# A 8192 x 8192 float32 transpose: column strips with staggered store windows and 16 KB SBUF runs

## The chip, the cores and the metric

The kernel runs on one core of one Trainium2 chip. The metric is the device time of one execution in microseconds (us), as the median over runs. The profile is of one execution of the program, taken by the hardware profiler.

A core has a matrix engine (TensorE, PE in the profile), two engines that copy here (VectorE, DVE, and ScalarE, ACT), GpSimd (POOL), which only builds an identity matrix, and SyncE (SP), which here only issues transfers. Data moves between the off-chip memory (HBM) and the on-chip memory (SBUF, 128 partitions) through 16 DMA engines. TensorE writes its results into a small memory of its own, PSUM, from which an engine has to copy them into SBUF.

## The reference

```
def setup_inputs():
    return {
        "x": np.random.randn(8192, 8192).astype(np.float32),
    }

def reference(x: np.ndarray) -> np.ndarray:
    return np.transpose(x)
```

The input has 268.44 MB, and so has the output. Every byte is read once from HBM and written once to it.

## The kernel before

The matrix is cut into blocks of 1024 rows by 2048 columns (`I` by `J`); there are 8 by 4 of them. The outer loop runs over the column blocks, the inner one over the row blocks. A block is one input tile `in_tile` of 128 partitions by 8 rows by 2048 columns (64 KB in each partition). Two of them take turns. It is loaded by two transfers of 4 MB on SyncE's queue (L55): each takes four groups of 128 rows, and a partition receives from each group one run of 8 KB.

The block is then worked off in four groups of four column slices. For each column slice of 128 columns, TensorE transposes eight squares of 128 x 128 (L63) into a PSUM tile `ps` of 128 x 1024, with the identity as the other operand. Four such PSUM tiles, of two banks each, take turns. A whole PSUM tile is copied into a quarter of an `out_tile`, alternately by ScalarE (L69) and VectorE (L71). When four quarters are there, ScalarE's queue issues one store of 2 MB (L76). In it, each partition holds four output rows of 1024 elements, so each run is 4 KB both in SBUF and in HBM; the four rows of a partition lie 128 output rows (4 MB) apart. Four `out_tile` buffers take turns.

All semaphores and the buffers' addresses are chosen by the tile framework. An engine waits where its next instruction needs a tile that is not there or not free: a load waits for the transposes of the block two before it, a transpose waits for the copy that frees its PSUM tile, a copy waits for the store that frees its `out_tile`. The loads have SyncE's queue to themselves; the stores share ScalarE's instruction stream with half of the copies.

Of the kernel before, what the change touches and what calls it, by code (L numbers as in the profile page):

```python
# [1 line left out]

# [5 lines left out]


@with_exitstack
def kernel(
    ctx: ExitStack,
    tc: tile.TileContext,
    x: bass.AP,
    out: bass.AP,
):
    nc = tc.nc
    P = 128
    N, M = x.shape  # L20
    assert x.shape == out.shape[::-1]

    dt = x.dtype

    R = 8
    C = 16
    I = R * P
    J = C * P
    G = 4
    LS = 2  # L30

    const_pool = ctx.enter_context(tc.tile_pool(name="const", bufs=1))
    in_pool = ctx.enter_context(tc.tile_pool(name="in_pool", bufs=2))
    out_pool = ctx.enter_context(tc.tile_pool(name="out_pool", bufs=4))
    psum_pool = ctx.enter_context(tc.tile_pool(name="psum", bufs=4, space=bass.MemoryType.PSUM))

    ident = const_pool.tile([P, P], dt)
    make_identity(nc, ident)

    n_bi = N // I  # L40
    n_bj = M // J

    copy_idx = 0

    for bj in range(n_bj):
        j0 = bj * J
        for bi in range(n_bi):
            i0 = bi * I

            in_tile = in_pool.tile([P, R, J], dt)  # L50
            rs = R // LS
            for s in range(LS):
                src = x[i0 + s * rs * P:i0 + (s + 1) * rs * P, j0:j0 + J]
                src = src.rearrange("(a p) j -> p a j", p=P)
                nc.sync.dma_start(out=in_tile[:, s * rs:(s + 1) * rs, :], in_=src)  # L55

            for g in range(C // G):
                out_tile = out_pool.tile([P, G, I], dt)
                for bb in range(G):
                    b = g * G + bb  # L60
                    ps = psum_pool.tile([P, R * P], dt)
                    for a in range(R):
                        nc.tensor.transpose(  # L63
                            ps[:, a * P:(a + 1) * P],
                            in_tile[:, a, b * P:(b + 1) * P],
                            ident,
                        )
                    if copy_idx % 2 == 0:
                        nc.scalar.copy(out=out_tile[:, bb, :], in_=ps)  # L69
                    else:  # L70
                        nc.vector.tensor_copy(out=out_tile[:, bb, :], in_=ps)  # L71
                    copy_idx += 1

                dst = out[j0 + g * G * P:j0 + (g + 1) * G * P, i0:i0 + I]
                dst = dst.rearrange("(b q) i -> q b i", q=P)
                nc.scalar.dma_start(out=dst, in_=out_tile)  # L76


# [1 line left out]
_INS = ['x']  # L80
_OUTS = [((8192, 8192), 'float32')]


# [23 lines left out]
```

## Time and profile before

| What | Value |
|---|---|
| Median of 10 runs | 1278.55 us (1277.35 to 1280.78) |
| Profiled execution, device time | 1280.58 us |
| Profiled execution, span from first to last instruction | 1278.8 us |
| Mean granted TensorE clock | 0.732 of full speed |
| TensorE matmul busy | 702.9 us (55%), 4096 instructions |
| VectorE busy | 313.5 us (25%), 256 instructions |
| ScalarE busy | 252.9 us (20%), 257 instructions |
| DMA, moved over the span | 537.49 MB, mean 420 GB/s |

Busy time is the sum over an engine's own instructions; an engine that waits is not busy. The DMA rows count packets, the pieces in which the 16 DMA engines move data; a queue's share is the time that its packets took, as a share of 16 times the span. The queue q1 carries the loads and q10 the stores. "Idle before" in a group's row is the time for which its engine stood still just ahead of it, with what released it. In the row of slices the span is cut into 40 equal parts, and 9 means busy for 90% or more.

### The profile page before, as it was taken

How to read it: one execution, taken by the hardware profiler on the slowest of the kernel's cores; microseconds unless marked ns; L12 is line 12 of the kernel's file. 1: busy time of each engine (PE TensorE's matmuls, PEld its weight loads, DVE VectorE, ACT ScalarE, POOL GpSimd, SP SyncE). 2: the span in 40 equal slices, each digit the busy share in tenths (PEclk: the TensorE clock that was granted, in tenths of full speed). 3: DMA queues.
4: the chain of work that ended last, by engine and by line, in shares of the span. 5: the costliest groups of instructions: out<-in, count | busy, mean ns of one | idle time of the engine just before them, and what ended most of it. 6: DMA issues, size and time to landing. Idle time of an engine off the chain costs nothing.

```text
span 1278.8 us, 9511 instructions
## 1 busy us (share of the span) xinstructions
PE 702.9 (55%) x4096; PEld 632.4 (49%) x4096; DVE 313.5 (25%) x256; ACT 252.9 (20%) x257; POOL 0.7 (0%) x6
## 2 busy tenths in 40 slices
PE   4565556555565545655456555465554655556553
PEld 3454445454455544645446444464544655445453
DVE  1222223222232212222122222222222222222222
ACT  1221112121121212212122121212212122121211
POOL 0000000000000000000000000000000000000000
PEclk8767777766777677786677776877667776777767
DMA  9999999999999999999999999999999999999998
GB/s 393 425 422 425 424 424 425 422 423 422 424 423 422 423 424 424 423 422 420 425 424 422 423 424 424 423 422 423 421 425 423 422 423 422 424 423 422 423 422 342
DMA packets 101418, 537.49 MB, mean 420 GB/s; under 512 B 3072, under 2 KB 3072, under 8 KB 68608
## 3 DMA queue, kind: packets, MB, share of 16 engines
q10 hardware_dynamic: 67584, 268.44, 51.3%
q1 hardware_dynamic: 33792, 268.44, 49.6%
q8 instruction: 32, 0.52, 0.1%
q14 instruction: 10, 0.08, 0.0%
HBM read 268.44 MB, written 268.44 MB: 420 GB/s over the span
## 4 chain that ended last, share of the span: by engine, by line
DMA 89%; PE 6%; DVE 3%; issue 0%; ACT 0%; DVEq 0%; ACTq 0%; SPq 0%
DMA out_dram<-out_tile 87%; PE ps L63 6%; DVE out_tile L71 3%; DMA in_tile<-in_x_dram 2%; ACT out_tile L69 0%; DVEq L71 0%; ACTq L69 0%; SPq L55 0%
## 5 line engine op out<-in xcount | busy, mean ns | idle before, releaser
L63 PE MATMUL ps<-ident,in_tile 128*128 128x128 f32 x4096 | 702.9, 345 | 559.9 <-DVE out_tile L71 534.6
L63 PEld LDWEIGHTS ps<-ident,in_tile 128*128 128x128 f32 x4096 | 632.4, 182 | 630.1 <-DVE out_tile L71 603.8
L71 DVE COPY out_tile<-ps 128x1024 f32<-128x1024 f32 x256 | 313.5, 1225 | 950.5 <-DMA out_dram<-out_tile 596.7
L69 ACT COPY out_tile<-ps 128x1024 f32<-128x1024 f32 x256 | 251.6, 1014 | 1008.6 <-DMA out_dram<-out_tile 845.1
L69 ACT ACT_TABLE_LOAD x1 | 1.3, 1283 | 0.7 <-PEq L91 0.7
masks.py:199 POOL TENSOR_SCALAR_AFFINE_SELECT ident<-ident 128x128 f32<-128x128 f32 x1 | 0.3, 292 | 0.1
masks.py:197 POOL MEMSET ident<- 128x128 f32 x1 | 0.2, 204 | 0.3 <-POOLq L91 0.3
L91 POOL MEMSET const-bfloat16-1.0<- 128x1 bf16 x1 | 0.1, 101 | 0.0
L91 POOL MEMSET const-uint8-127<- 128x1 uint8 x1 | 0.1, 101 | 0.0
L91 POOL MEMSET const-float32-0.0<- 128x1 f32 x1 | 0.1, 98 | 0.2 <-issue 0.2
L91 POOL MEMSET const-float32-1.0<- 128x1 f32 x1 | 0.1, 98 | 0.0
## 6 DMA issues: line engine op xcount, KB each, us to landing
in_tile<-in_x_dram SPq DMA_DIRECT2D x64, 4096.0 KB, 28.0
out_dram<-out_tile ACTq DMA_DIRECT2D x128, 2048.0 KB, 29.3
```

The source lines that it names most:

```text
L63: nc.tensor.transpose(ps[:, a * P:(a + 1) * P], in_tile[:, a, b * P:(b + 1) * P], ident,)
L69: nc.scalar.copy(out=out_tile[:, bb, :], in_=ps)
L71: nc.vector.tensor_copy(out=out_tile[:, bb, :], in_=ps)
L91: nc = _bacc.Bacc("TRN2", target_bir_lowering=False, num_devices=1)
```

## The change

The program is written anew, with fixed buffers and hand-placed semaphores inside one critical section of the framework. The computation per square (a TensorE transpose, then a copy out of PSUM) stays.

- The matrix is cut into two strips of 4096 columns. A strip is read in 64 chunks of 128 rows: one load of 2 MB per chunk, 16 KB per partition in one run. Three input buffers take turns.
- A chunk has 32 squares, in eight groups `q` of four (`B = 4`). The four squares of a group go into one PSUM bank of 128 x 512; eight banks take turns. Even groups are copied by ScalarE, odd ones by VectorE.
- Each group collects its squares in a region of SBUF (`reg`, 16 KB per partition; nine of them) over a window of eight chunks. The windows of the eight groups are staggered by one chunk: at the start of a strip group 0's window has one chunk, group 1's two, and so on; after that one group closes at every chunk. At the last chunk of a strip all eight close.
- When a group closes, its region is stored: 128 partitions, four output rows each, of 4 KB for a full window. The SBUF side of the store is described as one run of 16 KB per partition, the HBM side as four rows of 4 KB (`wide_dma`). The first store alone is an ordinary one.
- Loads and stores are all issued by SyncE, on one queue. In its order of instructions, a chunk's store comes ahead of the load of the chunk three later.
- A tensor `pad` of 128 B per partition is placed ahead of the identity and the buffers.

```diff
+def physical(ap):
+    t = ap.tensor
+    dims = [list(d) for d in ap.ap]
+    if len(dims) == 2:
+        dims.insert(1, [dims[1][1], 1])
+    return mybir.PhysicalAccessPattern(
+        ap=dims, offset=ap.offset, dtype=ap.dtype,
+        memref=t.name, memsetref=t.name + "_set",
+    )
+
+def wide_dma(nc, eng, queue, out, in_):
+    return eng.add_instruction(
+        mybir.InstDMACopy(
+            mode="Copy",
+            name=nc.get_next_instruction_name(),
+            engine=eng.engine,
+            ins=[physical(in_)],
+            outs=[physical(out)],
+            queue=queue,
+        )
+    )
...
-    R = 8
-    C = 16
-    I = R * P
-    J = C * P
-    G = 4
-    LS = 2
...
+    S = 32
+    B = 4
+    W = 8
+    NR = S // B
+    NIN = 3
+    NREG = 9
+    NPS = 8
+    CH = N // P
+    J = S * P
+
+    with tc.tile_critical():
+        nc.alloc_sbuf_tensor("pad", [P, 32], dt)
+        ident = nc.alloc_sbuf_tensor("ident", [P, P], dt).ap()
+        ins = [nc.alloc_sbuf_tensor(f"in{k}", [P, J], dt).ap() for k in range(NIN)]
+        regs = [nc.alloc_sbuf_tensor(f"reg{k}", [P, B * W * P], dt).ap() for k in range(NREG)]
+        pss = [nc.alloc_psum_tensor(f"ps{k}", [P, B * P], dt).ap() for k in range(NPS)]
...
+        chunks = [(s, c) for s in range(M // J) for c in range(CH)]
+
+        def load(t):
+            s, c = chunks[t]
+            nc.sync.dma_start(
+                out=ins[t % NIN], in_=x[c * P:(c + 1) * P, s * J:(s + 1) * J]
+            ).then_inc(s_ld[t % NIN], 16)
+
+        for t in range(NIN):
+            load(t)
...
+        for t, (s, c) in enumerate(chunks):
+            nc.tensor.wait_ge(s_ld[t % NIN], 16 * (t // NIN + 1))
+            closing = []
+            for q in [(c + k) % NR for k in range(NR)]:
+                if q not in window:
+                    end = min(c + (q - c) % W, CH - 1)
+                    r = free.pop(0)
+                    window[q] = (c, end, r)
+                    if stored[r]:
+                        (nc.scalar, nc.vector)[q % 2].wait_ge(s_st[r], 16 * stored[r])
+                c0, end, r = window[q]
+                rows = (end - c0 + 1) * P
+                view = regs[r][:, :B * rows].rearrange("p (b i) -> p b i", b=B)
+                ps = pss[n % NPS]
+                e = q % 2
+                if bank[n % NPS] is not None:
+                    nc.tensor.wait_ge(*bank[n % NPS])
+                for b in range(B):
+                    last = nc.tensor.transpose(
+                        ps[:, b * P:(b + 1) * P],
+                        ins[t % NIN][:, (q * B + b) * P:(q * B + b + 1) * P],
+                        ident,
+                    )
+                last.then_inc(s_pe, 1)
+                n += 1
+                o = view[:, :, (c - c0) * P:(c - c0 + 1) * P]
+                i = ps.rearrange("p (b i) -> p b i", b=B)
+                (nc.scalar, nc.vector)[e].wait_ge(s_pe, n)
+                if e == 0:
+                    cp = nc.scalar.copy(out=o, in_=i)
+                else:
+                    cp = nc.vector.tensor_copy(out=o, in_=i)
+                cp.then_inc(s_cp[e], 1)
+                copied[e] += 1
+                bank[(n - 1) % NPS] = (s_cp[e], copied[e])
+                if c == end:
+                    closing.append((q, e, copied[e]))
+            for q, e, count in closing:
...
+                nc.sync.wait_ge(s_cp[e], count)
+                if stores:
+                    st = wide_dma(nc, nc.sync, "qSPDynamicHW", dst, regs[r][:, :B * rows])
...
+                st.then_inc(s_st[r], 16)
...
+                free.append(r)
+            if t + NIN < len(chunks):
+                nc.sync.wait_ge(s_pe, n)
+                load(t + NIN)
```

## The prediction

> **What bounds the kernel now.** I read the page's slices and DMA queues first, then the chain and the waits, then the DMA view in three windows: loads alone, the steady middle, stores alone.
>
> ```profile
> DMA  9999999999999999999999999999999999999998
> DMA packets 101418, 537.49 MB, mean 420 GB/s; under 512 B 3072, under 2 KB 3072, under 8 KB 68608
> q10 hardware_dynamic: 67584, 268.44, 51.3%
> q1 hardware_dynamic: 33792, 268.44, 49.6%
> DMA out_dram<-out_tile 87%; PE ps L63 6%; DVE out_tile L71 3%; DMA in_tile<-in_x_dram 2%; ACT out_tile L69 0%; DVEq L71 0%; ACTq L69 0%; SPq L55 0%
> L63 PE MATMUL ps<-ident,in_tile 128*128 128x128 f32 x4096 | 702.9, 345 | 559.9 <-DVE out_tile L71 534.6
> L71 DVE COPY out_tile<-ps 128x1024 f32<-128x1024 f32 x256 | 313.5, 1225 | 950.5 <-DMA out_dram<-out_tile 596.7
> ```
>
> The 16 DMA engines are full from the first slice to the last. The chain is 87% stores. VectorE (DVE) waits 596.7 us for stores to free `out_tile`; TensorE (PE) waits 534.6 us for VectorE. All waiting ends at the DMA engines, so compute counts for nothing until it exceeds its cover. The only ways down are less engine time for each byte, and less idling at the two ends.
>
> The queue rows give the price of a packet: q1 (loads) 0.496 x 16 x 1278.8 us over its 32768 packets of 8 KB (the other 1024 are the small ones, 16 per DMA, counted as nothing) is 309.7 ns; q10 (stores) likewise 160.2 ns for each of 65536 packets of 4 KB. Two 4 KB packets cost 320.4, so a packet carries a fixed part: 2 x 160.2 - 309.7 = 10.7 ns. Records overlap a little (the shares add to 100.9%), so I also take it from rates. The next three answers are windows 6 to 22, 640 to 960 and 1250 to 1270 us:
>
> ```profile
> DMA packets 853, 6.80 MB, mean 425 GB/s; under 512 B 23, under 2 KB 23, under 8 KB 23
> ...
> DMA packets 25606, 135.37 MB, mean 423 GB/s; under 512 B 777, under 2 KB 777, under 8 KB 17403
> ...
> DMA packets 2103, 8.37 MB, mean 418 GB/s; under 512 B 63, under 2 KB 63, under 8 KB 2102
> ```
>
> Loads alone run at 425 GB/s, or 16 x 8192 / 425 = 308.4 ns a packet; stores alone at 418, or 156.8 ns; the fixed part is 5.2 ns. The ends, windows 0 to 24 and 1262 to 1279 us, 40 slices each:
>
> ```profile
> GB/s 0 0 0 259 341 423 423 437 437 423 437 437 410 437 410 410 423 437 423 437 437 423 423 423 410 437 423 423 437 423 437 410 410 423 410 423 437 410 410 423
> ...
> GB/s 424 386 443 434 395 414 434 414 405 424 424 424 414 414 424 424 386 443 434 395 395 318 289 251 174 125 135 135 125 106 96 67 58 58 29 19 19 0 0 0
> ```
>
> The start loses 2.2 us (9.27 MB moved by 24 us, which take 21.8 at 425). The end loses 6.1 us: the last 17 us move 4.57 MB, 10.9 us of work at 420, because the 16 engines run dry one after another. So 8.3 us are ends, and 1270.5 us are 537.49 MB at 423 GB/s.
>
> **The change, part by part.**
>
> Descriptors. A load of 16 KB runs has 1024 packets per engine instead of 2048 (268.44 MB / 16 / 16384); stores that read 16 KB runs have 1024 reads per engine where there were 4096, with four written rows to each. Price of a 16 KB packet: from the rates, 4 x (308.4 - 156.8) + 5.2 = 611.6 ns; from the records, 4 x (309.7 - 160.2) + 10.7 = 608.7 ns. Neither knows of alignment, which the diff changes too: ahead of the old tiles lie four constants of 32 B and the identity's 512 B per partition, so by my count they start 128 B past a multiple of 256; the `pad` of 128 B makes that 256.
>
> Here the Trainium skill decides between the two. "DMA: Bandwidth & Descriptors", in "Why small descriptors are slow" and "How a descriptor splits into AXI transactions", counts 32 B beats: about 3 cycles on top for each packet, and for a start off a 256 B boundary the beats of the bytes before it, here 4. At the 850 MHz of "Where 436 GB/s comes from" that is 135 beats = 158.8 ns for 4 KB and 263 = 309.4 ns for 8 KB. The trace's 160.2 and 309.7 agree to 1%, though it can't say how much of the fixed part is alignment. By the rule an aligned 16 KB packet is 515 beats = 605.9 ns, by the trace's rates alone 611.6; the page's ceiling of 435 GB/s, an estimate for the lower end, is 602.4. I take 605.9, since it explains both rows, and keep both ends. 2048 packets x 605.9 = 1240.9 us of full engines (1233.7 to 1252.6), against 1270.5 now.
>
> More, smaller DMAs. Loads go from 64 of 4 MB to 128 of 2 MB. Stores go from 128 to 142: per strip one closes at each of chunks 0 to 62, and eight at chunk 63. So 270 DMAs against 192. A rule speaks against this: "SBUF — State Buffer", "The DMA setup-cost knee", puts about 2 us on every DMA; 78 more in series would add 156 us. The row: the window from 6 to 22 us holds the seam between the first and second load of one queue and still averages 425, and four store seams fit in the 418. So a seam costs nothing while something is queued behind it; the small packet at each end of a DMA is at most 78 x 10.7 ns = 0.8 us, which I add.
>
> Short stores. The staggered windows make 28 of the 142 stores short, with rows of 512 B to 3.5 KB (29.4 MB in all). They write 896 rows per engine where full rows would be 448: 448 x 5.2 = 2.3 us if each row is paid, 0 if only the read run is. I take 1, and keep 0 to 5, since no row of the trace shows 512 B writes.
>
> One queue. Stores move from ScalarE's queue (ACTq, 0.38 us an issue) to SyncE's, behind a wait for the closing copy; behind each store waits the next load. 270 issues at 0.4 to 0.9 us are up to 240 of 1250 us for SyncE, free of the path. The load for chunk t+3 goes when PE has done chunk t. When a load lands, its ring still holds two stores and two loads (8 MB, 19 us at 423). PE has 5.8 us of busy time per chunk (702.9 / 4096 = 172 ns x 32); even at the slow pace the timeline shows (24 transposes in 4.54 us) it is 6.1 us. So at least 10 us of queue remain, and PE, 32 transposes per 9.7 us, stays under 65%. Copies are halved in width and doubled in number: 1225 / 2 and 1014 / 2 ns plus some 60 ns, four each per chunk, under 3 us. The PSUM handoffs, now 1024 over eight single banks with hand-written waits, and the ninth store region are hidden by the same 10 us. The region needed by the last copy of a chunk is stored two chunks earlier and lands about 5 to 7 us into the chunk; that copy may wait 1 to 2 us, with only the next chunk's copies behind it.
>
> Strip change. Chunk 64 needs eight regions at once, held by the closing stores (36 x 256 KB = 9.4 MB, 22 us). PE stops, but two loads and those stores are in the ring, and when they end a third and fourth load (10 us) are there; PE catches up in about 3 us. Cost 0 (up to 5).
>
> Ends. First load at 0.7 us as now; chunk 0 lands at about 8 us and, at the timeline's first pace (16 transposes in 3.65 us), frees the next load at about 15.3, when the ring is full until 17: 0, with 2 us at risk. At the end 22 us of stores stand queued; the engines' unequal end stays: 6.1 us.
>
> Sum: 1240.9 + 0.8 + 1 + 8.3 = 1251.0 us of span. The profiled execution took 1280.58 for a span of 1278.8 (+1.8), the runs' median 1278.55 is 2.0 under that; so span and median are within 0.2: **1251 us**, 2.2% faster.
>
> **The rivals.** (1) Stores pay for each 4 KB row written, and alignment is worth nothing to them: 1024 x 605.9 + 4096 x 156.8 = 1262.7, plus 8.3, 0.8 and 2.3: 1274. For it: nothing in the trace shows a run that differs between its two sides. Against: the beat count fits, and aligned rows alone, at 152.1 ns, would already give 1254.
> (2) Slower: one ring for both directions. Before, loads and stores had a ring each; now each engine turns from reading HBM to writing it in one ring, 256 times. If a turn drains the ring, the gain of 27.5 us is gone from 0.11 us a turn; at 0.25 us the time is 1315. Against: the engines now alternate directions at nearly every packet, over 60,000 times, and 423 lies between 425 and 418. That those turns are between two rings leaves this open.
> (3) Loads starve in the first chunks or at the strip change: 5 to 15 us, so 1256 to 1266. My timeline leaves 2 us at the start and several later.
> (4) The wide store is split back into 4 KB descriptors: as (1), or 1254 with alignment.
>
> **How the numbers follow.** The likeliest case has 0.70 (1244 to 1262, from the bounds of the packet and the short stores); rivals 1 and 4 0.12, rival 3 0.08, rival 2 0.10. The range 1243 to 1274 takes in all but rival 2 and stragglers. A difference under 0.2% (2.6 us) can't be told from none; part of rival 1 falls there. Faster 0.86, same 0.04, slower 0.10.
>
> **What would show it.** Right: a load packet near 606 ns, 16384 load packets of 16 KB, about 431 to 433 GB/s in the middle, PE waiting for loads. Stores: few 16 KB packets at 432 (mine) or 4 KB packets near 157 (rival 1). Dips in GB/s at each seam mean rival 2; slices under 9 in the first 30 us or near 630, rival 3. I am wrong if the middle stays at or below 425.

## The result, and the profile after

The changed kernel takes 1266.05 us (median of 9 runs, 1265.58 to 1269.74) against 1278.6 us for the kernel before on the same chips (median of 31). The ratio is 0.9905, with a 95% interval of 0.9896 to 0.9913: 0.95% faster. Forecast were 1251 us and 2.2%. The direction was right and 1266 lies in the range of 1243 to 1274, but the gain is less than half of the forecast one. The profiled execution took 1265.90 us for a span of 1264.1 us.

First the page of the changed kernel: slices, DMA packets, the one queue, the chain, and two of the costliest groups.

```profile
DMA  9999999999999999999999999999999999999998
GB/s 380 418 429 428 429 428 430 428 428 428 427 429 428 429 430 431 427 429 429 428 416 428 430 428 429 430 429 430 428 428 429 430 429 429 427 430 429 430 430 355
DMA packets 39308, 537.51 MB, mean 425 GB/s; under 512 B 4320, under 2 KB 4832, under 8 KB 6240
q1 hardware_dynamic: 39264, 536.89, 100.0%
DMA in<-in_x_dram 76%; PE ps L131 20%; DMA out_dram<-reg 2%; DVE reg L144 0%; ACT reg L142 0%; SPq L197 0%; SPq L68 0%; ACTq L140 0%
L131 PE MATMUL ps<-ident,in 128*128 128x128 f32 x4096 | 726.2, 360 | 510.6 <-DMA in<-in_x_dram 495.7
L144 DVE COPY reg<-ps 128x512 f32<-128x512 f32 x512 | 353.5, 692 | 883.7 <-PE ps L131 850.6
```

The DMA engines are as full as before. What changed is the number of packets, 39308 for 101418, and the middle's rate. The waiting has turned round: TensorE now waits for loads (495.7 us of its 510.6 idle), where it waited for copies that waited for stores. That is a change of where the backlog stands, not of what bounds: one full set of DMA engines, before and after.

The rate of the middle, in a window without short stores or strip change (100 to 560 us), and the last 20 us of the span:

```profile
DMA packets 13541, 197.23 MB, mean 429 GB/s; under 512 B 1501, under 2 KB 1501, under 8 KB 1501
q1 hardware_dynamic: 13524, 196.99, 100.5%
```

```profile
GB/s 438 406 373 430 455 373 418 487 373 430 451 434 406 406 418 369 438 438 422 401 455 365 422 365 438 287 274 270 217 238 225 238 201 168 98 29 4 0 0 0
DMA packets 934, 6.33 MB, mean 316 GB/s; under 512 B 110, under 2 KB 110, under 8 KB 494
```

At 429 GB/s a packet of 16 KB takes 16 x 16384 / 429 = 611.0 ns of an engine, as a mean of loads and stores (611.4 with 197.23 MB in 460 us unrounded). All 537.51 MB at that rate are 1253 us; the remaining 11.1 us of the span are its ends and seams. The last 20 us lose 5.2 us of them (6.33 MB are 14.8 us of work), the first 24 us lose 3.6 (8.76 MB moved), the second slice 0.8 (418 against 429 over 31.6 us), and the 50 us from 610, around the strip change, 1.2 (20.94 MB moved).

So of the 13.1 us between forecast and measured span, 12.1 are the packets (1253 for 1240.9) and 1.0 the rest (11.1 for 10.1). The experiments ask about the packets first.

### The profile page after: what moved, and what is told of

Same layout as the page of the kernel before. It is cut to its first block, busy times and chain, and to the rows that moved or that the text cites. A ratio compares the mean times of both kernels' runs of the same rounds, so it can differ in the third digit from the quotient of the medians.

```text
span 1264.1 us, 9814 instructions
## 1 busy us (share of the span) xinstructions
PE 726.2 (57%) x4096; PEld 694.1 (55%) x4096; DVE 353.5 (28%) x512; ACT 300.5 (24%) x513; POOL 0.7 (0%) x6
## 2 busy tenths in 40 slices
DMA packets 39308, 537.51 MB, mean 425 GB/s; under 512 B 4320, under 2 KB 4832, under 8 KB 6240
## 4 chain that ended last, share of the span: by engine, by line
DMA 78%; PE 20%; issue 0%; DVE 0%; ACT 0%; SPq 0%; ACTq 0%
DMA in<-in_x_dram 76%; PE ps L131 20%; DMA out_dram<-reg 2%; DVE reg L144 0%; ACT reg L142 0%; SPq L197 0%; SPq L68 0%; ACTq L140 0%
## 5 line engine op out<-in xcount | busy, mean ns | idle before, releaser
L131 PE MATMUL ps<-ident,in 128*128 128x128 f32 x4096 | 726.2, 360 | 510.6 <-DMA in<-in_x_dram 495.7
L131 PEld LDWEIGHTS ps<-ident,in 128*128 128x128 f32 x4096 | 694.1, 194 | 542.5 <-DMA in<-in_x_dram 516.7
L144 DVE COPY reg<-ps 128x512 f32<-128x512 f32 x512 | 353.5, 692 | 883.7 <-PE ps L131 850.6
L142 ACT COPY reg<-ps 128x512 f32<-128x512 f32 x512 | 299.2, 585 | 936.2 <-PE ps L131 906.4
```

The costliest lines, as they stand in the source:

```text
L131: last = nc.tensor.transpose(ps[:, b * P:(b + 1) * P], ins[t % NIN][:, (q * B + b) * P:(q * B + b + 1) * P], ident,)
L142: cp = nc.scalar.copy(out=o, in_=i)
L144: cp = nc.vector.tensor_copy(out=o, in_=i)
```

## The experiments

Theory P, formed on seeing the result: a packet costs its bytes plus a fixed part (8 to 9 ns in the packet records), wherever it starts in SBUF. Its rival, theory B, is the prediction's count of beats, in which a start off a 256 B boundary costs 4 beats, 4.7 ns. The kernel before, run beside each group, had medians of 1277.8 to 1278.6 us, so groups can be compared to within a microsecond. Packet times called "recorded" are medians of the single packets in the trace; rates are from the DMA view. Which addresses are multiples of 256 is the prediction's count, since no trace shows an address; but theory B puts 4 beats between two starts that lie 128 B apart in any case.

### Alignment: the pad taken out, and put into the kernel before

```diff
-        nc.alloc_sbuf_tensor("pad", [P, 32], dt)
```

> The changed kernel without the 128 B pad, so that every tile starts 128 B past a multiple of 256. Theory P (a packet costs its bytes plus a fixed 8 to 9 ns, wherever it starts): same as the changed kernel, 1266 us within 2. Theory B (the prediction's beat count: 4 beats, 4.7 ns, for each packet that starts off the boundary): 2048 packets x 4.7 ns = 9.6 us more, 1275.7, and load packets of 616 ns where they are 611.

Measured: median 1274.08 us, but scattered from 1265.85 to 1277.51 over 9 runs (ratio to before 0.995, 0.9927 to 0.9972). The recorded packets are the same: medians of 611 ns for loads and 616 for stores. So theory B's charge on every packet is not there, and yet most runs are slower. Between 100 and 560 us the rate is 428. The loss shows in the slices, and in the last 20 us of this version:

```profile
GB/s 385 414 427 428 429 428 429 427 427 429 428 429 426 428 430 429 430 428 428 425 384 426 427 427 429 431 429 428 428 428 430 429 428 428 429 430 428 430 411 305
```

```profile
GB/s 369 397 422 520 434 459 336 336 520 455 332 451 385 467 385 401 393 389 422 418 397 401 352 369 45 33 16 33 25 25 25 25 25 25 25 20 4 0 0 0
```

Strip change 384 for 416, last slice 305 for 355. In the second row each number is half a microsecond: the rate falls at once to 25 GB/s and stays there for some 6 us. That is about the share of one engine of 16 (428 / 16 = 27), so by this reading one DMA engine has fallen behind and finishes alone. The middle, at 428, shows nothing of it; the loss appears where all engines have to be done, at the strip change and at the end.

The same pad in the kernel before:

```diff
+    pad = const_pool.tile([P, 32], dt)
+    nc.gpsimd.memset(pad, 0.0)
     ident = const_pool.tile([P, P], dt)
```

> The kernel before with 128 B put ahead of its identity, so that all its tiles start on a multiple of 256; nothing else. Theory P: no change, 1278.6 us, packets of 309 and 159 ns. Theory B: 4.7 ns less for each of 6144 packets, 28.9 us less, 1250, packets of 305 and 154 ns.

Measured: 1276.69 us (0.9984, 0.9975 to 0.9992), 1.7 us less than the kernel before beside it (1278.4), where theory B had 28.9. The recorded packets stay at 309 and 159 ns. The two runs together refute theory B's charge on every packet.

### Which side's alignment: loads or stores

Two versions misalign one side each, by another pad between the input buffers and the regions, or by moving the pad there.

```diff
         ins = [nc.alloc_sbuf_tensor(f"in{k}", [P, J], dt).ap() for k in range(NIN)]
+        nc.alloc_sbuf_tensor("pad2", [P, 32], dt)      # version "regions off"
         regs = [nc.alloc_sbuf_tensor(f"reg{k}", [P, B * W * P], dt).ap() for k in range(NREG)]
```

> The changed kernel with another 128 B between the input buffers and the regions: loads land on multiples of 256, stores read from 128 past one. Without any pad the time rose by some 8 us at equal packet times, with the loss at the strip change and the end. If the stores' reads are what lags: 1272 to 1276 with a decay of few engines at the end. If the loads' writes are: 1266.

Measured: 1266.47 us, 1265.83 to 1266.93, the changed kernel's time.

> The pad moved between the input buffers and the regions: loads land 128 past a multiple of 256, stores read from a multiple. If the loads' writes are what lags: 1272 to 1276. If the stores' reads are: 1266. If it takes both, or hangs on the identity's address: both mixed versions 1266.

Measured: 1272.47 us, scattered from 1266.73 to 1275.54, with the same end:

```profile
GB/s 524 496 471 389 356 336 582 397 336 430 418 467 319 516 344 430 430 414 352 430 397 377 258 16 33 33 16 33 25 25 25 25 25 25 20 25 4 0 0 0
```

So it goes with the loads, writing SBUF 128 B past a boundary; stores read from there at no cost that shows. In this version the identity has moved by 128 B too, as it had without the pad. No run moves the loads' buffers alone; but only TensorE reads the identity, and the lag is in the DMA engines. Why one engine and not all, the trace doesn't say.

### The stores' long reads undone

```diff
-                if stores:
+                if False:
                     st = wide_dma(nc, nc.sync, "qSPDynamicHW", dst, regs[r][:, :B * rows])
```

> The changed kernel with every store an ordinary one, whose SBUF side is four runs of 4 KB. Theory P: store packets of 4 KB at 159 ns, four of them 636 where one packet of 16 KB took 616 in the records; by the rates of before 4096 x 156.8 = 642.3 us against 1024 x some 612 = 627: 13 to 15 us more, about 1280. Theory B, in which alignment carried the stores' gain: 152 to 154 ns a packet and 0 to 4 us more, 1266 to 1270.

Measured: 1276.37 us (0.9983, 0.9975 to 0.9992), 10.3 us above the changed kernel. The middle (100 to 560 us):

```profile
DMA packets 31421, 195.46 MB, mean 425 GB/s; under 512 B 1491, under 2 KB 1491, under 8 KB 25488
```

425 for 429 over the whole is 537.51 MB x (1/425 - 1/429) = 11.8 us. The recorded 4 KB packets take 159 ns, aligned as they are. The stores' long reads are worth more than the loads' long runs, which come next.

### The loads' long runs undone, and both

```diff
-            nc.sync.dma_start(out=o, in_=i)
+            wide_dma(
+                nc, nc.sync, "qSPDynamicHW",
+                o.rearrange("p (h j) -> p h j", h=2),
+                i.rearrange("p (h j) -> p h j", h=2),
+            )
```

> The changed kernel with every load (but the first three) described as two runs of 8 KB per partition. Theory P: two packets of 309 ns for one of 611, by the rates 2 x 308.4 - 611.6 = 5.2 ns x 1024 = 5.3 us more, 1271.4. Theory B: 3 beats, 3.6 us more, 1269.7. A rival in which the run length of loads counts for nothing: 1266.

Measured: 1269.17 us (0.9926, 0.9915 to 0.9938), 3.1 us above the changed kernel; theory P's 5.3 is too much, and theory B's 3.6 is nearer. This run alone doesn't settle it; it shows that the loads' run length is worth something.

> The changed kernel with loads of 8 KB runs and ordinary stores of 4 KB runs: the packets of the kernel before, aligned, in the new order of work on one queue. Theory P (packet prices add): 1266.05 + 10.3 (ordinary stores, measured alone) + 3.1 (8 KB loads, measured alone) = 1279.5. If the windows, the short stores and the single queue cost nothing: 1276.7, what the aligned kernel before took.

Measured: 1281.29 us (1.0026, 1.0016 to 1.0036): 15.2 us above the change, a little over the 13.4 of the parts, and slower than the kernel before. Against the aligned kernel before, with the same full-size packets, it is 4.6 us more. That is the cost of the new order of work, short stores included. Its slices show where:

```profile
GB/s 378 411 423 424 423 424 423 424 423 423 422 424 424 423 423 425 425 424 424 422 409 421 424 423 423 425 425 423 423 424 425 424 423 425 424 424 425 424 423 352
```

The first two slices and the one at the strip change lie below the 424 of the others. The aligned kernel before, with the same early packets, has 390 and then 425 in its first two slices. So the change wins only by its packets; the strips and staggered windows that make them possible cost some of it.

### One ring or two

```diff
-                nc.sync.wait_ge(s_cp[e], count)
+                nc.scalar.wait_ge(s_cp[e], count)
-                    st = wide_dma(nc, nc.sync, "qSPDynamicHW", dst, regs[r][:, :B * rows])
+                    st = wide_dma(nc, nc.scalar, "qActDynamicHW", dst, regs[r][:, :B * rows])
```

> The changed kernel with its stores issued by ScalarE on its own queue, so that loads and stores have a ring each again. Rival of one ring (the prediction's rival 2, in a mild form): 2 to 5 us less, 1261 to 1264, if turning between directions in one ring costs 0.01 to 0.02 us a turn. Theory P: packets of 611 and 616 ns as before, 1266 within 1.5; a store goes out later in its chunk, behind ScalarE's copies, which the queue covers.

Measured: 1272.29 us, 1268.16 to 1273.56 (0.9951, 0.9939 to 0.9964). The middle has the same rate, and the two queues show the two prices:

```profile
DMA packets 13549, 197.30 MB, mean 429 GB/s; under 512 B 1505, under 2 KB 1505, under 8 KB 1505
q10 hardware_dynamic: 6767, 98.54, 50.4%
q1 hardware_dynamic: 6766, 98.54, 50.1%
```

Turning between directions in one ring costs nothing that can be seen: 429 with one ring and with two. With equal bytes, stores take 50.4% to the loads' 50.1% (recorded 615 and 611 ns).

The version is slower overall for another reason, and its slice at the strip change shows where: 353, where the changed kernel has 416. ScalarE spent 29.7 us there (613.2 to 642.9 us) in issuing the eight closing stores, and its copies stood behind them. Of its waits over the whole run, the two that show it:

```profile
ACT reg L142 <- issue: 29.2, 1, 29.2
PE ps L131 <- ACT reg L142: 38.0, 14, 29.3
```

SyncE takes as long over the same eight stores in the changed kernel (30.8 us from 604.1), but it has no copies to make. My expectation that the queue covers this was wrong at that one place. The profiled execution took 1269.08 us; what puts most of the others some 3 us higher is not traced.

### Four written rows against one

The stores write one row of 16 KB per partition.

```diff
-                dst = out[j0:j0 + B * P, c0 * P:c0 * P + rows]
-                dst = dst.rearrange("(b q) i -> q b i", q=P)
+                dst = out[g0:g0 + P, f0:f0 + B * rows]
```

> The changed kernel whose stores write one row of 16 KB per partition instead of four of 4 KB. It leaves out the placing of the four rows: the output holds the same bytes in other places. Theory P with a price per written row (616 ns against 611 in the records, 1.7 ns for each row after the first): store packets of 611 ns, 1024 x 5 ns = 5 us less, 1261. If the 5 ns are hidden or come from reading SBUF: 616 ns and 1266.

Measured: 1260.93 us (0.9868, 0.9856 to 0.9881), 5.1 us less, with 16 KB packets recorded at 611 ns, loads and stores alike. The middle (100 to 560 us) and the slices of this version are

```profile
DMA packets 13596, 198.05 MB, mean 431 GB/s; under 512 B 1506, under 2 KB 1506, under 8 KB 1506
GB/s 381 429 429 429 431 430 430 430 431 433 429 431 430 430 431 430 432 430 431 430 413 425 430 431 430 431 430 431 431 429 432 430 431 430 430 431 431 431 430 358
```

198.05 MB in 460 us are 608.9 ns for each 16 KB packet with one row on either side. The changed kernel has 611.4, and 2.5 ns x 2048 packets are 5.1 us: the whole difference is the price of the four rows.

The second slice is 429 where the changed kernel has 418. That alone looks like the price of short stores with four rows each. But the version with two rings makes the same short four-row stores and has 430 in that slice, so the 0.8 us need the one ring as well; why, these runs don't show.

### Longer runs: 32 KB with two buffers

```diff
-    B = 4
-    NIN = 3
-    NREG = 9
-    NPS = 8
+    B = 8
+    NIN = 2
+    NREG = 5
+    NPS = 4
```

(and windows staggered by two chunks).

> The changed kernel with eight squares per group: stores read 32 KB runs and write eight rows of 4 KB; four groups, staggered by two chunks; five regions of 32 KB; two input buffers instead of three, for the room. Theory P: a 32 KB packet takes 2 x 602.4 + 8.6 + 7 x 1.7 = 1225 ns, 612.6 for each 16 KB against 616: 1024 x 3.4 ns = 3.5 us less, 1262.5. Rival: two input buffers let the loads run dry, or the larger last stores lengthen the end: 1270 and more, with slices of DMA under 9 or an end that loses over 8 us where 5 are lost now.

Measured: 1359.96 us (1.0643, 1.0629 to 1.0657). The middle, 100 to 560 us, has lost 7% of its rate:

```profile
DMA packets 9484, 183.63 MB, mean 399 GB/s; under 512 B 1056, under 2 KB 1056, under 8 KB 1056
q1 hardware_dynamic: 9469, 183.41, 97.1%
```

The queue was occupied for 97.1% of the time, 100.5% in the changed kernel, so the ring running dry is about half of the loss. The other half is in packets that took longer: the 32 KB packets there have a median of 1218 ns, 7 under the expectation, but a mean of 1314. What held some of them up is not shown. TensorE's waits for loads grow to 733.4 us. Two input buffers alone:

> The changed kernel with two input buffers instead of three, nothing else: does the 32 KB version lose to its packets or to its two buffers? If two buffers are the cause: the ring runs dry, DMA slices under 9, TensorE waits for loads more than its 496 us, 1280 or more. If 16 KB stores, which come evenly one per chunk, leave cover enough: 1266 to 1268, and the 32 KB version lost to its 4 MB stores.

Measured: 1278.77 us, so 12.7 us over three buffers, a little under the first expectation's 1280 and without its dry ring in the middle. The middle stays at 428 GB/s; the loss lies at the start and the strip change:

```profile
GB/s 341 397 427 426 424 426 429 428 429 428 428 429 429 427 428 428 428 429 429 425 361 414 426 427 427 429 426 428 430 428 429 430 428 428 427 429 429 428 427 359
```

So the prediction was right that the middle has cover to spare: one buffer less leaves the ring full there. Two buffers alone, then, don't make the 32 KB version's dry middle, and the next version, with stores of 3.5 MB and three buffers, keeps 428 as well. It takes the large stores and the two buffers together.

### 28 KB with three buffers

```diff
-    B = 4
-    W = 8
+    B = 8
+    W = 7
-    NREG = 9
+    NREG = 5
```

> The changed kernel with eight squares per group and windows of seven chunks: stores read 28 KB runs and write eight rows of 3.5 KB; three input buffers again, five regions of 28 KB, one group closing every one or two chunks. Does the price per byte go on falling beyond 16 KB when the ring stays full? Theory P: 1054 + 8.6 + 5 to 15 ns (as the eight rows of 2 KB and of 4 KB cost) = 1068 to 1078 ns, 610 to 616 for each 16 KB against 616: 0 to 6 us less, 1260 to 1266. Rival: stores of 3.5 MB hold loads and regions back: DMA slices under 9 or a slower strip change and end, over 1268.

Measured: 1272.66 us (0.9957, 0.9945 to 0.9969), the rival's time. The recorded 28 KB packets have a median of 1078 ns, 616 for each 16 KB, as with four rows and 16 KB: eight rows take back what the longer run saves. The middle runs at 428, and the strip change (388) and the early slices (364, 410) are worse. Beyond 16 KB these versions had nothing left to win.

### Shorter rows, no strips

Three versions walk chunks of 128 full rows without strips. The first has groups of eight squares and windows of four chunks (rows of 2 KB), the second 32 squares and two chunks (1 KB rows, 32 KB runs), the third also loads full rows of 32 KB.

```diff
-        chunks = [(s, c) for s in range(M // J) for c in range(CH)]
+        steps = [(c, h) for c in range(CH) for h in range(H)]
-    B = 4
-    W = 8
+    B = 8     # second and third: 32
+    W = 4     # second and third: 2
```

> No strips: the matrix is walked in chunks of 128 full rows, each loaded as two halves of 4096 columns; groups of eight squares, windows of four chunks, so that a store reads 16 KB runs and writes eight rows of 2 KB. If the extra 5 ns of a store's packet are per packet, whatever the number of rows: 616 ns, and 1 to 2 us less for the strip change that is gone, 1264 to 1265. If they are 1.7 ns for each row after the first: 623 ns, 7 us more, 1271 to 1272. Short rows that HBM takes slowly would show as packets well over 623.

Measured: 1279.58 us (1.0006, 0.9998 to 1.0015). Store packets are recorded at 626 ns, 15 above the loads' 611: with eight rows the surcharge is three times that of four. The middle has 426 GB/s, which accounts for 8.8 us against 429. The first slices (376, 394) and the last (324) are worse too.

> No strips, halves of 4096 columns as above with four input buffers; groups of 32 squares, windows of two chunks: a store reads 32 KB runs and writes 32 rows of 1 KB. If the extra is per packet: 1218 ns (as the 32 KB packets with eight rows took where they weren't held up), 609 for each 16 KB, 7 us less than the change and 1 to 2 for the strips: 1257 to 1258. If 1.7 ns per row: 1266 ns, 17 us more, 1282.

> As the version with 1 KB rows, and loads of full rows: 32 KB runs, 4 MB each, three input buffers, three regions of 32 KB. Loads at 1213 ns for 32 KB, 606.7 for each 16 KB against 611: 4.4 us less on top, 1253, if the ring stays full. If a region that comes free late holds up the copies: DMA slices under 9 and 1270 or more; if rows are priced singly, 1278.

Measured: 1843.76 and 1852.09 us (1.4383 and 1.4492). The page of the second version:

```profile
DMA packets 31805, 537.51 MB, mean 291 GB/s; under 512 B 3089, under 2 KB 7185, under 8 KB 7185
q1 hardware_dynamic: 31760, 536.88, 97.0%
```

The engines are occupied 97.0% of the time and yet move only 291 GB/s: between 100 and 560 us the 32 KB store packets have a median of 1720 ns and a mean of 1897, and the 16 KB loads beside them a mean of 784, where the 16 KB packets of the changed kernel have 614. None of my expectations had this. A store here writes 32 rows of 1 KB, 4 MB apart in HBM, from one run; whether the shortness or the number of far rows does it, these runs don't separate.

No version that computes the transpose beat the changed kernel.

## Why the prediction was right or wrong

**What bounds.** Right. All slices of DMA stay at 9, TensorE ends at 57% busy and waits for loads.

**The price of a packet: the step that failed.** The prediction had two prices for 16 KB: 611.6 ns from the rates of the trace, and 605.9 ns from the beat count of the Trainium skill ("DMA: Bandwidth & Descriptors", "How a descriptor splits into AXI transactions"). It took the second "since it explains both rows", and it put the four written rows of a store at nothing. Measured are 611.0, the mean of loads and stores, so the term was 1240.9 us and came to 1253. Two parts make up the 12 us.

- About 6 to 7 us are the packet itself, 608.9 ns with one row on either side (the version with one row). The beat count agreed with both rows to 1% because 3 cycles for the packet and 4 beats for alignment add up to the fixed part. The two had not been seen apart, and the 4 beats that the change was to take away were not there: the pad in the kernel before is worth 1.7 us instead of 28.9. The same count with these beats left in is 519 beats, 610.6 ns, an estimate from the same section.
- About 5 us are the rows: written singly they cost 5.1 us.

The prediction's 611.6 looks right to 0.1%, and with it its own sum gives 1252.6 + 0.8 + 1 + 8.3 = 1262.7 us, against a measured span of 1264.1. Part of that is luck: as a price for a packet with one row it is 2.7 ns too high, and it leaves out 2.5 ns for the rows. Of the signs that it named, the middle at 431 to 433 and a load packet near 606 failed; 16 KB packets and TensorE waiting for loads came true.

**The wide store.** Right in kind: one packet per 16 KB read, with four rows. Undone, it costs 10.3 us. Rival 1 (stores pay for each row as for a packet) fell, though its remark that alignment is worth nothing to stores holds, and rows aren't free, as said above. Rival 4, a store split back, fell with the packet count.

**More, smaller DMAs on one queue.** Right. 270 DMAs in place of 192 leave the middle at the rate of its packets, and two rings give the same 429. The Trainium skill's rule of about 2 us for each DMA ("SBUF — State Buffer", "The DMA setup-cost knee") did not show for DMAs with others queued behind them. Rival 2, a price on turning in one ring, fell.

**Short stores, strip change, ends.** Short stores were put at 1 us; the second slice loses 0.8, which two rings would have avoided, so this agreement may be chance. The strip change was put at 0 with up to 5 and is 1.2. The start loses 3.6 where 2.2 were taken, the end 5.2 where 6.1 were. Rival 3, starving loads, stays small with three buffers; with two it costs 12.7 us, at the start and the strip change that the rival named. Together with the rest of the ends and seams these are 11.1 us for 10.1 forecast.

**What the sum left out.** In the experiment with the old packet sizes the new order of work is 4.6 us slower than the aligned kernel before. The prediction had 1.8 us for what is new (0.8 and 1). The 4.6 us take over a quarter of what the packets gain, 15.2.

## What to carry to other kernels

When the DMA engines are full, look at the bytes per packet on each side of a transfer. The SBUF side and the HBM side of one DMA can have runs of different lengths; reading four HBM rows' worth of SBUF as one run saved 10.3 us of 1276 here, and eight rows per run instead of four took it back.

When a stated rule and a rate from the trace give different prices, and the rule fits the rows only as a sum of two parts, keep to the rate until a run has shown the parts one by one. Then price what the trace has no example of, here several rows to one packet, by a run of its own.

## What the runs showed of the hardware that was not expected

- A load that writes SBUF from 128 B past a multiple of 256 (by count) doesn't take longer per packet (611 ns either way), but the kernel can end in a tail of some 6 us at 25 GB/s, the share of one of the 16 engines. Times were scattered (1265.85 to 1277.51 us). Stores that read from such addresses showed no effect (1266.47 us).
- Several rows written from one 16 KB read: four rows of 4 KB add 5 ns to 611, eight rows of 2 KB add 15. With 32 rows of 1 KB from one 32 KB read, 4 MB apart, the whole kernel fell to 291 GB/s.
- With the DMA queue full, issuing eight closing stores held the issuing engine for 29.7 us on ScalarE and 30.8 on SyncE. On SyncE that cost nothing; ScalarE had copies waiting behind it.
